# Forget-gate attention by head pairs: row sums by DMA, values held still, S5 and a merge's gates as filler

## The chip, the cores and the metric

The kernel runs on one core of a Trainium2 chip. The core has TensorE (PE, with its weight loads listed apart as PEld), VectorE (DVE), ScalarE (ACT), GpSimd (POOL) and SyncE (SP), which here only issues DMAs. The metric is the time of one execution on the device in microseconds; lower is better.

## The reference, cut to what matters

Two blocks run one after the other on a sequence of 512 tokens with 1024 features. The first block is two hybrid layers, each with neighbourhood attention (NA), grouped-query attention and spatial gating. The second block has forget-gate attention (fox), a state-space mixer (ssd) and a diagonal state-space mixer (S5), merged by gates, and a convolutional feed-forward part.

```python
def neighbourhood_attention(q, k, v, rpb):      # 8 heads of 64, grid 8 x 64
    scores = jnp.einsum('brqhd,brjkhd->bhrqjk', qg, kg) * (dh ** -0.5)
    scores = scores + bias                      # relative bias, window of 16 columns
    p = jax.nn.softmax(jnp.where(col_valid, scores, -1e30))
    out = jnp.einsum('bhrqjk,brjkhd->brqhd', p, vg)
...
def fox_attention(q, k, v, f_logit):            # 8 heads of 64, blocks of 128 queries
    cum = jnp.cumsum(jax.nn.log_sigmoid(f_logit), axis=1)
    for i in range(4):
        s = q[i] @ k[:, :q1].T * scale
        s = s + cum[:, :, q0:q1, None] - cum[:, :, None, :q1]
        p = jax.nn.softmax(jnp.where(causal, s, -inf))
        out = p @ v[:, :q1]
...
merged = sum over the three branches of sigmoid(gate_r + b_gate) * (y_r @ w_branch[r])
```

ssd needs, per head, the exponential of the differences of a running sum within chunks of 128 tokens (`exp(segsum(adt))`) and the exponential of the sum itself. S5 is a complex linear recurrence over the tokens.

## The kernel before, in words

Every large product is made in three parts. An operand is split into a rounded high half and a remainder, and `mm3` (L94) issues high x high (L99), high x remainder (L100, L101) into one PSUM tile. `load_w` (L67) brings a weight tile `wr` by an SP DMA, ScalarE rounds it to `wh` (L76), and DVE or POOL subtracts to get `wl` (L78); which of the two is told by the pattern `lo_gp`, one entry per tile in turn. An `fm_job` makes one output tile of 512 columns in four units of six products; the units wait in a queue and `fill(n)` (L165) takes n of them as filler between the steps of an attention. The tile scheduler then fixes the order on each engine, and each engine works its own queue in order.

NA (`na`, L590) works in 16 steps per layer, one for each pair of heads and 16 columns of queries. A step's scores for two heads are two products against a zero-padded high half of the keys with all 128 rows (L659) and two against the remainder with 64 rows each (L662). The keys of a step are 32 columns of 8 grid rows, taken with a stride. The values of two heads go into the column halves of one PSUM tile (L699).

Block 2 (`block2`, L1479) runs fox, ssd, merges 0, 1 and 2, with S5 (`s5`, L1363) as a generator that is advanced by `step`. RF, RS and RM say how much one call of `step` adds in fox, in ssd and in the merges: 0, 0.5 and 1.5. `fdt` (L829) makes the running sums `CS` of the gates and turns them token-major by small transposes (L862). In fox the 32 steps are one head and one block of 128 queries each. A step's scores are a product with all rows (L941), one with 64 rows (L942) and one that adds the causal mask as a product with the identity (L943). The running sum along the keys is spread over the partitions by a product with one column of the identity (L872, once per head) and copied by ScalarE (L937). A reduction on DVE (L947) subtracts it and finds the maximum; then come the exponential on ScalarE (L952) and the reciprocal on DVE (L953). `weights_T` transposes the weights on PE (L304); the values (L979) hold the transposed weights still and stream 64 columns of `v`, ScalarE scales the result by the reciprocal (L980), and the output of two heads is transposed back to features (L983) and copied (L984). ssd spreads its sums in the same way (L872, with a mask product L1070), and by a product with a selector matrix (L1089). In fox three of four `wl` are made by POOL, in the merges all of them. A merge (`merge_gen`, L716) makes, for each pair of output tiles, two gate jobs and a projection. S5's products with its state are L1438 and L1440, its sums L1394 to L1448. PSUM has three tiles for `mm`, two for `s`, two for `t` and one for `v`.

Of the kernel before, what the change touches and what calls it, by code (L numbers as in the profile page):

```python
# [14 lines left out]
ALU = mybir.AluOpType  # L15
# [10 lines left out]
class Net:  # L26
# [176 lines left out]
    def consts2(self):  # L203
        nc, a, cp = self.nc, self.a, self.cp
        self.identb = cp.tile([P, P], BF16, name="identb")
        nc.vector.tensor_copy(self.identb, self.ident)
        self.identr = cp.tile([P, P], F32R, name="identr")
        nc.vector.tensor_copy(self.identr, self.ident)
# [111 lines left out]
    def heads_k(self, src):  # L320

        nc, out, lo = self.nc, [], self.b2(F32R)
        for s in range(2):
            r, o = slice(64 * s, 64 * s + 64), slice(64 - 64 * s, 128 - 64 * s)
            k = self.b2(F32R)
# [3 lines left out]
            out.append(k)  # L329
        return out, lo  # L330
# [259 lines left out]
    def na(self, l, vd):  # L590
# [12 lines left out]
        def kj(hp):  # L603
            def use(ps):
                kf = self.tmp()
                nc.scalar.activation(kf, ps, AF.Identity, bias=self.col(f"b{l}", 4 + hp))
                kzs[hp] = self.heads_k(kf)
            return self.fm_job(fm[4 + hp], use)
# [14 lines left out]
        def load(hp):  # L623
            vw = [self.b2(shape=(P, 4, P)) for _ in range(2)]
            vr = vd.rearrange("(r c) f -> r c f", c=64)
            for j in range(4):
                for half in range(2):
                    nc.sync.dma_start(vw[j // 2][:, 2 * (j % 2) + half], vr[4 * half:4 * half + 4, LO[j]:LO[j] + 32, hp * P:hp * P + P])
            vws[hp] = vw
            bts[hp] = []  # L630
            for s in range(2):
                t = self.ld(shape=(P, 8, 48))
# [3 lines left out]
        def bias(i):  # L636
# [7 lines left out]
            bms[i] = self.b2(shape=(P, 2, 8, 32))  # L644
            x0 = (16, 8, 8, 0)[j]
            for s in range(2):
                nc.gpsimd.tensor_tensor(bms[i][:, s], bts[hp][s][:, :, x0:x0 + 32],  # L647
                                        self.namask[:, (0, 1, 1, 2)[j], None].to_broadcast([P, 8, 32]), op=ALU.add)

        def weights(hp, j):  # L650
# [12 lines left out]
            for s in range(2):  # L663
                nc.vector.tensor_tensor_reduce(out=e[:, s], in0=pss[s], in1=bm[:, s].rearrange("p r c -> p (r c)"), op0=ALU.add, op1=ALU.max,
# [1061 lines left out]
```

## Time and profile before

| | before |
|---|---|
| median of 3 runs | 2041.87 us (2039.82 to 2045.49) |
| the profiled execution | 2042.89 us |
| its span | 2041.1 us |
| mean granted clock, share of the upper level | 0.991 |
| PE busy | 1988.1 us (97%) |
| DVE, ACT, POOL busy | 1236.0, 863.2, 509.8 us (61%, 42%, 25%) |

The profiled execution has a span of 2041.1 us, and its own time is 1.8 us longer. The two hybrid layers take it to about 1134 us, fox with its head to 1325 us, ssd to about 1380 us, merges 0 and 1 to 1493 us; then come the last merge, the projection and the feed-forward part. A row of the timeline starts with the time from the start of the span; since matmuls are pipelined, what one costs is read from one start to the next.

### The profile page before, as it was taken

The numbers are of one execution on the slowest core, as the hardware profiler recorded it, in microseconds if no ns is written. First come the engines' busy times: TensorE is split into PE (matmuls) and PEld (weight loads), VectorE is DVE, ScalarE is ACT, GpSimd is POOL, SyncE is SP. The second block draws the span as 40 slices with busy tenths as digits, with TensorE's granted clock in tenths as the row PEclk, the third lists the DMA queues.
The fourth block names the chain that finished last, engine by engine and source line by source line (L and its number), as shares of the span: only waits on it lengthen the run. The fifth ranks groups of instructions, "written<-read, shape, count | busy, mean of one in ns | idle before, by whom it ended". The sixth has DMA issues, their size and how long they took to land. (4 is left out here: it accounts for less than half of the span.)

```text
span 2041.1 us, 29326 instructions
## 1 busy us (share of the span) xinstructions
PE 1988.1 (97%) x10594; PEld 1653.3 (81%) x10594; DVE 1236.0 (61%) x2406; ACT 863.2 (42%) x1738; POOL 509.8 (25%) x594
## 2 busy tenths in 40 slices
PE   7999999999999999999999999998899999999998
PEld 7898877788799988777878877877688888888888
DVE  7776655766477766567545644365425477635655
ACT  3445446433235554564332466542233334423431
POOL 3343321100633436323610222235440000000000
PEclk9999999999999999999999999999899999999999
DMA  6432223333352322334353412143433423333332
GB/s 207 153 106 67 80 89 105 109 93 122 117 167 89 105 75 78 124 109 140 107 159 115 140 63 62 62 131 105 138 98 108 130 83 100 102 93 99 98 86 70
DMA packets 140464, 218.54 MB, mean 107 GB/s; under 512 B 19232, under 2 KB 44576, under 8 KB 140320
## 3 DMA queue, kind: packets, MB, share of 16 engines
q1 hardware_dynamic: 140320, 216.68, 33.7%
q8 instruction: 83, 1.36, 0.3%
q14 instruction: 61, 0.50, 0.1%
HBM read 196.70 MB, written 19.92 MB: 106 GB/s over the span
## 5 line engine op out<-in xcount | busy, mean ns | idle before, releaser
L76 ACT CAST wh<-wr 128x512 fp32r<-128x512 f32 x605 | 362.1, 618 | 587.5 <-PE psmm L100 273.7
L99 PE MATMUL psmm<-xh,wh 128*128 128x512 f32 (+1 forms) x1504 | 604.3, 402 | 1.5 <-DVE b L373 1.4
L100 PE MATMUL psmm<-xl,wh 128*128 128x512 f32 (+1 forms) x1504 | 588.1, 391 | 0.3 <-DVE xl L262 0.3
L101 PE MATMUL psmm<-xh,wl 128*128 128x512 f32 (+1 forms) x1504 | 587.4, 391 | 0.2 <-DVE wl L78 0.2
L78 DVE TENSOR_TENSOR wl<-wr,wh 128x512 fp32r<-128x512 f32 x526 | 374.6, 723 | 348.9 <-ACT wh L76 341.4
L101 PEld LDWEIGHTS psmm<-xh,wl 128*128 128x128 f32 x1504 | 283.5, 189 | 61.6 <-DVE wl L78 1.8
L99 PEld LDWEIGHTS psmm<-xh,wh 128*128 128x128 f32 x1504 | 284.1, 189 | 60.8 <-issue 3.4
L100 PEld LDWEIGHTS psmm<-xl,wh 128*128 128x128 f32 x1504 | 284.4, 189 | 52.7 <-DVE xl L262 0.7
L247 POOL TENSOR_TENSOR sm<-sm,mhalf 128x1 f32<-128x1 f32 x20 | 18.9, 947 | 648.4 <-DVE sm L245 648.4
L78 POOL TENSOR_TENSOR wl<-wr,wh 128x512 fp32r<-128x512 f32 x79 | 109.7, 1401 | 229.2 <-ACT wh L76 228.7
L99 PE MATMUL psmm<-wh,xh 128*128 128x256 f32 (+1 forms) x512 | 148.3, 291 | 2.0 <-DVE b L373 1.3
L100 PE MATMUL psmm<-wl,xh 128*128 128x256 f32 (+1 forms) x512 | 147.1, 287 | 2.0 <-DVE wl L78 1.8
L101 PE MATMUL psmm<-wh,xl 128*128 128x256 f32 (+1 forms) x512 | 147.3, 288 | 0.4 <-DVE xl L262 0.4
L465 POOL TENSOR_SCALAR b<-b,sm 128x512 f32<-128x512 f32 x64 | 101.1, 1580 | 163.6 <-DVE sm L296 158.4
L99 PE MATMUL psmm<-b,wh 128*128 128x512 f32 x304 | 119.8, 394 | 0.0
L100 PE MATMUL psmm<-b,wh 128*128 128x512 f32 x304 | 118.6, 390 | 0.0
L101 PE MATMUL psmm<-b,wl 128*128 128x512 f32 x304 | 118.5, 390 | 0.0
L99 PEld LDWEIGHTS psmm<-wh,xh 128*128 128x128 f32 x512 | 99.4, 195 | 4.0 <-DVE b L373 1.7
L100 PEld LDWEIGHTS psmm<-wl,xh 128*128 128x128 f32 x512 | 99.5, 194 | 3.8 <-DVE wl L78 2.6
L101 PEld LDWEIGHTS psmm<-wh,xl 128*128 128x128 f32 x512 | 99.4, 194 | 0.9 <-DVE xl L262 0.9
L647 POOL TENSOR_TENSOR b<-ld,namask 128x256 f32<-128x256 f32 x48 | 42.7, 916 | 151.0 <-PE psv L699 57.3
L294 ACT ACTIVATE b<-pss,sm 128x512 f32<-128x512 f32 x64 | 44.1, 689 | 81.5 <-DVE sm L291 81.0
(393 smaller groups left out, 3304.3 us busy)
## 6 DMA issues: line engine op xcount, KB each, us to landing
wr<-in_w1fm SPq DMA_DIRECT2D x192, 256.0 KB
wr<-in_w2fm SPq DMA_DIRECT2D x92, 256.0 KB
wr<-in_wup SPq DMA_DIRECT2D x88, 256.0 KB
wr<-in_wbr SPq DMA_DIRECT2D x72, 256.0 KB
wr<-in_w1tm SPq DMA_DIRECT2D x56, 256.0 KB
wr<-in_wout SPq DMA_DIRECT2D x48, 256.0 KB
wr<-in_wdown SPq DMA_DIRECT2D x43, 256.0 KB
ld<-in_rows SPq DMA_DIRECT2D x32, 256.0 KB
```

Source lines behind the costliest of these rows:

```text
L76: nc.scalar.copy(hi[:, c], raw)
L78: eng.tensor_tensor(lo[:, c], raw, hi[:, c].bitcast(F32), op=ALU.subtract)
L99: mm(ps, wh, xh, start=(first and k == 0), stop=False)
L100: mm(ps, wh, xl, start=False, stop=False)
L101: mm(ps, wl, xh, start=False, stop=(last and k == n - 1))
L247: nc.gpsimd.tensor_tensor(rs, ve, self.mhalf[:, :1], op=ALU.pow)
L294: nc.scalar.activation(e[:, :n], src, AF.Exp, bias=nm, scale=scale, accum_out=sm)
L465: nc.gpsimd.tensor_scalar(e, e, r, None, op0=ALU.mult)
L647: nc.gpsimd.tensor_tensor(bms[i][:, s], bts[hp][s][:, :, x0:x0 + 32], self.namask[:, (0, 1, 1, 2)[j], None].to_broadcast([P, 8, 32]), op=A ...
```

## The change

NA stores the keys column by column, so that a step's 256 keys lie side by side, and keeps the remainder in both halves of the partitions, so that all four score products have 128 rows. The bias table and the values are laid out to match.

Fox works in 16 steps of two heads. Score products are four with all rows. `CS` is written to memory and spread by DMA (`bcast_row`); POOL subtracts the causal mask from the spread row (`sums`), and after the block on the diagonal has been read, POOL copies the unmasked block over it. The weights are scaled by POOL before they are transposed. The values hold `v` still, 64 columns for each head in the two column halves, and stream the transposed weights, so the output comes out by features. ssd takes its spread rows by DMA and its mask by a POOL addition; the selector product is a DMA to 64 partitions each.

S5 is advanced in fox as well (RF 0.5, from a start of -7) and at 0.5 in merges, with one more stop in it. All `wl` of fox, ssd and merges are made by DVE. The eight gate jobs of merge 0 stand in the filler queue during ssd, and are drained before merge 0. The jobs in fox are put in another order: S5's inputs early, the convolutions (`xj`) late.

```diff
-        nc, out, lo = self.nc, [], self.b2(F32R)
+        nc, out = self.nc, []
         for s in range(2):
             r, o = slice(64 * s, 64 * s + 64), slice(64 - 64 * s, 128 - 64 * s)
-            k = self.b2(F32R)
+            k, lo = self.b2(F32R), self.b2(F32R)
             nc.scalar.copy(k[r], src[r])
             nc.scalar.copy(k[o], src[r])
             nc.vector.tensor_tensor(lo[r], src[r], k[r].bitcast(F32), op=ALU.subtract)
-            out.append(k)
-        return out, lo
+            nc.scalar.copy(lo[o], lo[r].bitcast(F32))
+            out.append((k, lo))
+        return out
...
-            vr = vd.rearrange("(r c) f -> r c f", c=64)
+            vr = vd.rearrange("(r c) f -> c r f", c=64)
             for j in range(4):
                 for half in range(2):
-                    nc.sync.dma_start(vw[j // 2][:, 2 * (j % 2) + half], vr[4 * half:4 * half + 4, LO[j]:LO[j] + 32, hp * P:hp * P + P])
+                    c0 = LO[j] + 16 * half
...
-            jq = slice(j * P, j * P + P)
-            q, (ks, kl) = [x[:, jq] for x in qs[hp]], kzs[hp]
-            ks, (kl,) = ([x.rearrange("p (r c) -> p r c", c=64)[:, :, LO[j]:LO[j] + 32] for x in xs] for xs in (ks, (kl,)))
+            jq, jk = slice(j * P, j * P + P), slice(8 * LO[j], 8 * LO[j] + 256)
             pss = [self.psum("s", (P, 256)) for _ in range(2)]
             for s in range(2):
-                nc.tensor.matmul(pss[s], q[s], ks[s], start=True, stop=False)
+                for i, k in enumerate(kzs[hp][s]):
+                    nc.tensor.matmul(pss[s], qs[hp][s][:, jq], k[:, jk], start=(i == 0), stop=(i == 1))
             for s in range(2):
-                r = slice(64 * s, 64 * s + 64)
-                nc.tensor.matmul(pss[s], q[s][r], kl[r], start=False, stop=True)
...
-        js, ts = [], {}
+        js, done, ts = [], ts, ts or {}
 
...
         for dp in range(4):
-            js += [gj(2 * dp), gj(2 * dp + 1), pj(dp)]
+            js += ([] if done else [gj(2 * dp), gj(2 * dp + 1)]) + [pj(dp)]
         yield from self.jobs(js)
+
+    def gate_job(self, ts, dt, r, gates, bname, b0, buf):
+        def use(ps):
+            ts[dt] = buf()
+            self.nc.scalar.activation(ts[dt], ps, AF.Tanh, bias=self.hcol(bname, b0 + 8 * r + dt), scale=0.5)
+        return self.fm_job(gates(8 * r + dt), use)
...
+        self.csd = self.dr.tile([40, 512], F32, name="csd")
+        nc.sync.dma_start(self.csd, CS[0:40])
+        yield
...
+    def bcast_row(self, out, r):
+
+        self.nc.sync.dma_start(out, self.csd[r:r + 1].to_broadcast([out.shape[0], 512]))
...
-        js += [uj(F) for F in range(4)]
+        js += [xj(0), qj(1), kj(1), uj(0), uj(1), qj(2), kj(2), xj(1), uj(2), qj(3), kj(3), uj(3), xj(2), xj(3), xj(4), xj(5)]
+        js += [zj(i) for i in range(4)]
         self.queue.append(self.jobs(js))
         self.fill(12)
+        fdt = self.fdt(fd)
+        next(fdt)
+        self.lo_gp = (0,)
         self.fill(8)
+        next(fdt)
+        steps = [(hp, t) for hp in range(4) for t in range(4)]
...
+        def sums(hp):
+
+            cks[hp] = []
+            for s in range(2):
+                c, m = self.b2(), self.b2()
+                self.bcast_row(c, 2 * hp + s)
+                nc.gpsimd.tensor_tensor(m.rearrange("p (t q) -> p t q", t=4), c.rearrange("p (t q) -> p t q", t=4),
+                                        self.causal[:, None].to_broadcast([P, 4, P]), op=ALU.subtract)
+                cks[hp].append((c, m))
+        sums(0)
+        self.fill(6)
...
+            pss = [self.psum("s") for _ in range(2)]
+            es = [self.b2() for _ in range(2)]
+            for s in range(2):
+                qt, (kh, kl) = q[hp][s][:, t * P:t * P + P], kz[hp][s]
+                nc.tensor.matmul(pss[s][:, :nn], qt, kh[:, :nn], start=True, stop=False)
+                nc.tensor.matmul(pss[s][:, :nn], qt, kl[:, :nn], start=False, stop=True)
+
+            mx, nm, sm, r = (self.small(2) for _ in range(4))
+            for s in range(2):
+                c, m = cks[hp][s]
+                nc.vector.tensor_tensor_reduce(out=es[s][:, :n], in0=pss[s][:, :n], in1=m[:, :n], op0=ALU.subtract, op1=ALU.max,
+                                               scale=1.0, scalar=-3e38, accum_out=mx[:, s:s + 1])
+                if t < 3:
+                    nc.gpsimd.tensor_copy(m[:, n - P:n], c[:, n - P:n])
+            cq = self.cc[:, t, 2 * hp:2 * hp + 2]
+            nc.vector.scalar_tensor_tensor(nm, mx, -1.0, cq, op0=ALU.mult, op1=ALU.subtract)
             nc.vector.tensor_tensor(nm, nm, cq, op=ALU.add)
-            nc.scalar.activation(e[:, :n], e[:, :n], AF.Exp, bias=nm, accum_out=sm)
+            for s in range(2):
+                nc.scalar.activation(es[s][:, :n], es[s][:, :n], AF.Exp, bias=nm[:, s:s + 1], accum_out=sm[:, s:s + 1])
             nc.vector.reciprocal(r, sm)
-            return e, r
+            for s in range(2):
+                nc.gpsimd.tensor_scalar(es[s][:, :n], es[s][:, :n], r[:, s:s + 1], None, op0=ALU.mult)
+            return es
...
+                sc[i] = weights(hp, t)
+            self.fill(1)
+            step(1)
             self.fill(1)
             step(1)
             j = i - 1
             if 0 <= j < len(steps):
-                pes[j] = self.weights_T(sc[j][0], steps[j][1] + 1)
+                pes[j] = [self.weights_T(e, steps[j][1] + 1) for e in sc.pop(j)]
             self.fill(1)
             step(1)
             j -= 1
...
-                nc.scalar.mul(yt[:, s], po[:, s], sc.pop(j)[1])
-                if s:
-                    pt = self.psum("t", (P, P))
-                    nc.tensor.transpose(pt, yt.rearrange("p s d -> p (s d)"), self.ident)
-                    nc.scalar.copy(ys[hp][:, t * P:t * P + P], pt)
-                    if t == 3:
-                        self.d(f"fox_{hp}", ys[hp])
+                    for s in range(2):
+                        h = 2 * hp + s
+                        nc.tensor.matmul(po[64 * s:64 * s + 64], v[k][:, h * 64:h * 64 + 64], pe[s][:, k], start=(k == 0), stop=(k == t))
+                nc.scalar.copy(ys[hp][:, t * P:t * P + P], po)
...
+        def sums(j):
+
+            out = [self.b2() for _ in range(3)]
+            for s in range(2):
+                self.bcast_row(out[s], 32 + 2 * j + s)
+                nc.gpsimd.tensor_tensor(out[s], out[s], self.causalT, op=ALU.add)
+                self.bcast_row(out[2][64 * s:64 * s + 64], 32 + 2 * j + s)
+            return out
+        nxt = sums(0)
...
-        due = [0.0]
+        due = [-7.0]
...
+        self.queue.append(self.jobs([self.gate_job(ts, dt, 0, lambda i: a["w2fm"][22 + i], "bg", 0, self.b2) for dt in range(8)]))
         yb = self.ssd(xb, zz, lambda n: step(RS))
+        self.fill(drain=True)
         tags[:] = "s", "t"
-        self.lo_gp = (1,)
-        merge(0, ya, RM, first=True)
+        merge(0, ya, RM, first=True, ts=ts)
         merge(1, yb, RM)
...
-RF = 0.0
+RF = 0.5
 RS = 0.5
-RM = 1.5
+RM = 0.5
```

On PE in a fox step, before: the values of one head (L979), then its scores (L941 to L943) and, two filler products later, the output transpose (L983).

```order
L101 MATMUL psmm_13081<-xh_11669,wl_12881 128x512
L979 MATMUL psv_13099<-acc_76,b_2833_13091 128x64
L979 MATMUL psv_13099<-acc_77,b_2833_13091 128x64
L941 MATMUL pss_13148<-b_2762_12846,b_2735_12751 128x512
L942 MATMUL pss_13148<-b_2761_12845,b_2735_12751 128x512
L943 LDWEIGHTS identb
L943 MATMUL pss_13148<-causalb,identb 128x128
L99 MATMUL psmm_13172<-xh_11669,wh_12982 128x512
L100 MATMUL psmm_13172<-xl_11670,wh_12982 128x512
L983 MATMUL pst_13145<-ident,yt_13100 128x128
L101 MATMUL psmm_13172<-xh_11669,wl_12983 128x512
```

After, at the like place: scores of two heads in four full products (L950, L951); further on S5's output products (L1454, L1456), the two heads' transposes (L300) and their values side by side (L996).

```order
L950 MATMUL pss_13181<-b_2723_12731,b_2700_12651 128x512
L951 MATMUL pss_13181<-b_2724_12732,b_2700_12651 128x512
L950 MATMUL pss_13182<-b_2725_12737,b_2701_12654 128x512
L951 MATMUL pss_13182<-b_2726_12738,b_2701_12654 128x512
L99 MATMUL psmm_13164<-xh_11689,wh_12946 128x512
...
L1454 MATMUL psmm_13222<-b_2746_12816,ld_12985 128x128
L1456 MATMUL psmm_13222<-b_2811_13071,ld_12981 128x127
L1456 MATMUL psmm_13222<-b_2812_13072,ld_12982 128x127
L300 MATMUL pst_13241<-ident,b_2821_13088 128x128 x2
L300 MATMUL pst_13247<-ident,b_2822_13089 128x128 x3
L996 MATMUL psv_13270<-b_2836_13147,acc_76 64x128
L996 MATMUL psv_13270<-b_2838_13152,acc_76 64x128
```

The scores stand together, the mask product and the output transpose are gone, and S5's products stand inside the loop. Transposes of both heads stand together too.

On DVE in the last head pair of fox, before: the reduction (L947), the small instructions (L950 to L953), and little between them.

```order
L947 ISA b_3055_13870,sm_13871<-pss_13866,b_3001_13690 128x384
L947 ISA sm_13871 128x1
L950 TENSOR_SCALAR sm_13872<-sm_13871,cc 128x1
L951 TENSOR_TENSOR sm_13872<-sm_13872,cc 128x1
L953 RECIPROCAL sm_13874<-sm_13873 128x1
L914 SCALAR_TENSOR_TENSOR b_3062_13898<-tmp_13899,psmm_13843 128x512
L947 ISA b_3066_13912,sm_13913<-pss_13908,b_2984_13634 128x512
L947 ISA sm_13913 128x1
L950 TENSOR_SCALAR sm_13914<-sm_13913,cc 128x1
```

After: the reductions (L956), small instructions (L961, L962, L965) with convolution sums (L1012, L904), S5's sums (L1440, L1441) and a `wl` between them.

```order
L956 ISA b_3031_13919,sm_13925<-pss_13917,b_2924_13499 128x384
L956 ISA sm_13925 128x1
L904 SCALAR_TENSOR_TENSOR b_3014_13856<-tmp_13861,b_3014_13856 128x512
L956 ISA b_3032_13920,sm_13925<-pss_13918,b_2926_13503 128x384
L956 ISA sm_13925 128x1
L1440 TENSOR_TENSOR b_3039_13960<-b_3002_13815,ld_13560 128x512
L961 SCALAR_TENSOR_TENSOR sm_13926<-sm_13925,cc 128x2
L1012 SCALAR_TENSOR_TENSOR b_3037_13952<-psmm_13892,hcols,b_3037_13952 128x511
L962 TENSOR_TENSOR sm_13926<-sm_13926,cc 128x2
L1441 TENSOR_TENSOR b_3041_13962<-b_3004_13817,ld_13561 128x512
L1012 SCALAR_TENSOR_TENSOR b_3037_13952<-psmm_13892,hcols,b_3037_13952 128x510
L78 TENSOR_TENSOR wl_13978<-wr_13979,wh_13977 128x512
```

Between two pairs' reductions DVE now has some ten other large instructions, where before it had none or one.

On PE in merge 1, before: the wait for S5 lies here, at L1440 among products of the merge.

```order
L100 MATMUL psmm_15086<-xl_11670,wh_14997 128x512
L101 MATMUL psmm_15086<-xh_11669,wl_14998 128x512
L1440 MATMUL pst_14843<-b_3278_14801,ld_14785 128x127
L99 MATMUL psmm_15086<-xh_11669,wh_14997 128x512
L100 MATMUL psmm_15086<-xl_11670,wh_14997 128x512
L101 MATMUL psmm_15086<-xh_11669,wl_14998 128x512
L99 MATMUL psmm_15086<-xh_11669,wh_14997 128x512
L1440 MATMUL pst_14843<-b_3279_14802,ld_14786 128x127
L1438 MATMUL pst_14843<-b_3150_14258,ld_14789 128x128
L1440 MATMUL pst_14843<-b_3278_14801,ld_14785 128x127
```

After: S5's last products (L1456) stand in ssd, beside its own (L1111); further on merge 0 begins with three tiles at once behind the last gate job.

```order
L1101 MATMUL pst_14543<-b_3157_14437,b_3133_14371 64x128
L1101 MATMUL pst_14543<-b_3158_14438,b_3133_14371 64x128
L1454 MATMUL psmm_14560<-b_2962_13637,ld_14255 128x128
L1456 MATMUL psmm_14560<-b_3147_14410,ld_14251 128x127
L1456 MATMUL psmm_14560<-b_3148_14411,ld_14252 128x127
L1111 MATMUL pst_14580<-b_3154_14426,st_14291 64x128 x2
...
L100 MATMUL psmm_14915<-xl_11690,wh_14851 128x512
L101 MATMUL psmm_14915<-xh_11689,wl_14852 128x512
L99 MATMUL psmm_14988<-b_3234_14942,wh_14958 128x512
L99 MATMUL psmm_15002<-b_3234_14942,wh_14958 128x512
L99 MATMUL psmm_15026<-b_3234_14942,wh_14968 128x512
```

S5's products moved from the merges to fox and ssd.

## Rows read from the trace of the kernel before

**Rows 1.** The page, busy time of each engine over the span.

```profile
PE 1988.1 (97%) x10594; PEld 1653.3 (81%) x10594; DVE 1236.0 (61%) x2406; ACT 863.2 (42%) x1738; POOL 509.8 (25%) x594
```

**Rows 2.** PE's waits: line <- releaser: us in total, times, longest us.

```profile
PE pst L1440 <- POOL b L1427: 15.7, 3, 6.2
...
PE pst L862 <- DVE b L859: 3.6, 1, 3.6
```

**Rows 3.** Windows: S5 wait in merge 1, a full-DVE stretch, fox loop.

```profile
core 0: us, PE busy (x) PEld busy (x) DVE busy (x) ACT busy (x) POOL busy (x), PEclk, DMA share, GB/s
1424.00:1437.00 13.00, 6.78 (x31) 5.64 (x31) 9.52 (x8) 0.53 (x2) 8.47 (x6) 0.74 0.42 136
...
403.00:433.00 30.00, 30.00 (x151) 23.84 (x150) 28.17 (x88) 13.11 (x22) 0.21 (x2) 1.00 0.28 83
...
1170.00:1325.00 155.00, 153.91 (x798) 120.14 (x796) 67.06 (x212) 94.08 (x229) 33.35 (x26) 1.00 0.19 58
```

**Rows 4.** Timeline of PE, one step of neighbourhood attention: start us, us, instruction.

```profile
338.41 0.40 PE L101 MATMUL psmm<-xh,wl 128*128 128x512 f32 x1
338.74 0.66 PE L699 MATMUL psv<-b,b 128*64 128x128 f32 x8
339.33 0.51 PE L659 MATMUL pss<-b,b 128*128 128x256 f32 x2
339.77 0.39 PE L662 MATMUL pss<-b,b 64*128 64x256 f32 x2
340.08 0.50 PE L99 MATMUL psmm<-xh,wh 128*128 128x512 f32 x1
```

**Rows 5.** Timeline of PE, one fox step with 384 columns.

```profile
1229.38 0.56 PE L979 MATMUL psv<-acc,b 128*128 128x64 f32 x4
1229.74 0.42 PE L941 MATMUL pss<-b,b 128*128 128x384 f32 x1
1230.09 0.44 PE L942 MATMUL pss<-b,b 64*128 64x384 f32 x1
...
1230.50 0.48 PE L99 MATMUL psmm<-xh,wh 128*128 128x512 f32 x1
1230.81 0.40 PE L100 MATMUL psmm<-xl,wh 128*128 128x512 f32 x1
```

**Rows 6.** Timeline of PE, broadcast of a row sum in fox.

```profile
1172.39 0.63 PE L872 MATMUL pss<-b,identr 128*128 128x512 f32 x2
1172.86 0.39 PE L99 MATMUL psmm<-xh,wh 128*128 128x512 f32 x1
```

**Rows 7.** Timeline of PE, broadcast and mask in ssd.

```profile
1340.29 0.71 PE L872 MATMUL pss<-b,identr 128*128 128x512 f32 x2
1340.84 0.39 PE L1070 MATMUL pss<-causalTb,identb 128*128 128x512 bf16 x1
1340.88 0.58 PE L99 MATMUL psmm<-xh,wh 128*128 128x512 f32 x1
1341.30 0.39 PE L100 MATMUL psmm<-xl,wh 128*128 128x512 f32 x1
```

**Rows 8.** Lines on DVE by form, 1134 to 1500 us: busy us, mean ns | idle before.

```profile
L951 DVE TENSOR_TENSOR sm<-sm,cc 128x1 f32<-128x1 f32 x32 | 6.9, 214 | 0.9
...
L1430 DVE TENSOR_TENSOR b<-b,ld 128x512 f32<-128x512 f32 x4 | 5.9, 1480 | 0.0
...
L1394 DVE SCALAR_TENSOR_TENSOR b<-b,b 128x512 fp32r<-128x512 f32 x4 | 4.9, 1218 | 16.6 <-ACT b L1393 16.6
...
L1448 DVE SCALAR_TENSOR_TENSOR b<-b,b 128x512 f32<-128x512 f32 x4 | 2.8, 693 | 2.2 <-ACT b L1447 2.1
...
L1429 DVE TENSOR_TENSOR b<-b,ld 128x512 f32<-128x512 f32 x4 | 2.7, 680 | 0.0
```

**Rows 9.** Lines by form, 100 to 200 us, on POOL and on DVE.

```profile
L465 POOL TENSOR_SCALAR b<-b,sm 128x512 f32<-128x512 f32 x18 | 28.2, 1569 | 39.2 <-DVE sm L296 39.2
...
L78 DVE TENSOR_TENSOR wl<-wr,wh 128x512 fp32r<-128x512 f32 x26 | 18.1, 710 | 1.9 <-ACT wh L76 1.7
```

More of the change, by code (lines that the diff above doesn't have):

```diff
@@ L714, in merge, with merge_gen @@
         return out
-    def merge_gen(self, out, r, ys, wbr, gates, bname, b0, first=False, last=False, step=None):
+    def merge_gen(self, out, r, ys, wbr, gates, bname, b0, first=False, last=False, step=None, ts=None):
         nc = self.nc
@@ L865, in fdt @@
         nc.vector.tensor_copy(cc, pc)
-        self.CSr, self.cc = self.split(CS), cc
-    def bcast_row(self, ps, r, last=True):
-        one = self.identr[:, r:r + 1].to_broadcast([P, P])
-        for i in range(2):
-            self.nc.tensor.matmul(ps, one, self.CSr[i], start=(i == 0), stop=(i == 1 and last))
+        self.cc = cc
+        yield
+    def bcast_row(self, out, r):
+        self.nc.sync.dma_start(out, self.csd[r:r + 1].to_broadcast([out.shape[0], 512]))
     def fox(self, xb, zz, step):
@@ L915, in zj @@
             return self.fm_job(fm[8 + i], use)
-        js += [zj(i) for i in range(4)]
         def uj(F):
@@ L920, in fox @@
         self.ub = {}
-        js += [uj(F) for F in range(4)]
+        js += [xj(0), qj(1), kj(1), uj(0), uj(1), qj(2), kj(2), xj(1), uj(2), qj(3), kj(3), uj(3), xj(2), xj(3), xj(4), xj(5)]
+        js += [zj(i) for i in range(4)]
         self.queue.append(self.jobs(js))
         self.fill(12)
-        self.fdt(fd)
-        self.lo_gp = (1, 1, 1, 0)
+        fdt = self.fdt(fd)
+        next(fdt)
+        self.lo_gp = (0,)
         self.fill(8)
-        steps = [(hp, t, s) for hp in range(4) for t in range(4) for s in range(2)]
@@ L955, in fox @@
+            return es
         for i in range(len(steps) + 2):
             if i < len(steps):
-                hp, t, s = steps[i]
+                hp, t = steps[i]
                 while kz[hp] is None:
                     self.fill(1)
-                sc[i] = weights(hp, t, s)
+                if t == 2 and hp < 3:
+                    sums(hp + 1)
+                sc[i] = weights(hp, t)
+            self.fill(1)
+            step(1)
             self.fill(1)
@@ L1065, in ssd @@
                 mt = []
+                *pbs, e = nxt
+                nxt = sums(j + 1) if j < 3 else None
                 for s in range(2):
                     h = 2 * j + s
-                    pb = self.psum("s")
-                    self.bcast_row(pb, 32 + h, last=False)
-                    nc.tensor.matmul(pb, self.identb, self.causalT, start=False, stop=True)
-                    m = self.b2()
+                    m = pbs[s]
                     for c in range(4):
-                        nc.scalar.activation(m[:, c * P:c * P + P], pb[:, c * P:c * P + P], AF.Exp, bias=ncs[:, c, h:h + 1])
+                        nc.scalar.activation(m[:, c * P:c * P + P], m[:, c * P:c * P + P], AF.Exp, bias=ncs[:, c, h:h + 1])
                     nc.vector.tensor_tensor(m, m, cb, op=ALU.mult)
@@ L1086, in ssd @@
                 step(1)
-                pe = self.psum("s")
-                for i in range(2):
-                    nc.tensor.matmul(pe, pselr[:, j * P:j * P + P], self.CSr[i], start=(i == 0), stop=(i == 1))
-                e = self.b2()
-                nc.scalar.activation(e, pe, AF.Exp)
+                nc.scalar.activation(e, e, AF.Exp)
                 po = self.psum("t")
@@ L1434, in s5 @@
             yield
+            yield
             py = self.psum(tags[1])
@@ L1610, in _constants @@
     c["rst"] = r
-    ps = np.zeros((P, S), np.float32)
-    for j in range(4):
-        for s in range(2):
-            ps[32 + 2 * j + s, j * P + 64 * s:j * P + 64 * s + 64] = 1
-    c["psel"] = ps
     return c
```

76 lines of the change are left out of this document (24 added, 52 removed).

## The prediction

> **What bounds the kernel now.** I read the engine totals first, then what TensorE (PE) waited for, then busy time stretch by stretch, then single rows of PE's timeline. PE is busy for 1988.1 of 2041.1 us [rows 1]; every other engine has slack on the whole. So only two things can pay: less work on PE, or less waiting of PE. The waits are few [rows 2]: three waits of the S5 output products (L1440) for GpSimd (POOL), 15.7 us together, and one of the transposes in `fdt` (L862), 3.6 us. The stretch around one of the S5 waits shows that they cost more than they last: of 13 us PE worked 6.78, and its mean granted clock was 0.74 of the upper level, 2.4 GHz [rows 3]. In the forget-gate (fox) loop, 1170 to 1325 us, PE is full (153.91 of 155), while VectorE (DVE) is busy for 67.06 and POOL for 33.35 [rows 3]. That DVE slack is what the change spends.
>
> **The sum is made against the profiled execution**, 2042.9 us with a span of 2041.1; the median of the runs is 2041.9, so the profiled one stands 1 us high, which I neglect. What follows is in PE time, since PE is the end of nearly every stretch.
>
> **Neighbourhood attention, 32 steps (16 in each of two layers).** A step's scores take 0.44 us for the two products with all 128 rows (339.33 to 339.77), 0.31 for the two with 64 rows [rows 4], and the product after a 64-row one takes 0.31 [rows 5] instead of the 0.23 that 512 columns cost in an unbroken stream (0.47 for two [rows 6]): 0.83 us. After, four full products of 256 columns: at half of 0.23 each, so 0.46 by columns, and about 0.10 for coming out of the column-split value products, which is inside today's 0.44. That is 0.56, a gain of 0.27 a step and **8.8 us** in all. The extra copy of the low half falls to ScalarE, which works a small part of any such stretch. If that copy came late it would cost once per head pair, not per step: 8 times some 0.6 us at most, and I take nothing.
>
> **`fdt`.** Its transposes now stand eight products later in PE's order: 8 x 0.23 = 1.8 us of its 3.6 us wait go [rows 2, 6]. A shorter wait also costs less clock afterwards; by the S5 stretch a wait cost up to 13 x 0.26 = 3.4 us of it [rows 3], and I count half of that. **3.4 us** between 1.8 and 7.
>
> **Fox, scores.** A step for one head with 384 columns: 0.35 for the full product (1229.74 to 1230.09), 0.41 to the next ordinary product and 0.08 more in that [rows 5], 0.84 us; by the same reading 0.73 with 256 columns and 0.96 with 512. 16 x 0.73 + 8 x 0.84 + 8 x 0.96 = 26.1 us. After: 16 head pairs with four full products each, 16 x 4 x mean 0.16 us (columns in proportion to 0.23 for 512) = 10.2. Gain **15.9**.
>
> **Fox, values.** Today 160 small products at close to 0.1 each (four in 0.36 [rows 5], a little more in longer rows), 15.3 us, and 16 output transposes with the slower product behind them, 1.8. After, the two heads run abreast, as today's L699 does: eight products in 0.59 us, of which some 0.15 are entering and leaving [rows 4], so 160 in 8.8, and 16 entries and exits at 0.2 (a product before L699 holds the array for 0.33 instead of 0.23 [rows 4], and leaving costs the like), 3.2. Gain 17.1 - 12.0 = **5.1**. Head pairs also halve the places where softmax transposes interrupt the stream, 16 x 0.09 = **1.4**.
>
> **Row sums.** Eight pairs of broadcast products at 0.47 [rows 6] leave fox, **3.8**. In the state-space part (ssd) eight pairs at 0.55 go, eight mask products that make the next one 0.42 instead of 0.23, and four pairs of selector products: 4.4 + 1.9 + 2.0 = **8.3** [rows 7]. What replaces them is DMA on SyncE's queue and POOL work; 24 transfers there stand among weight loads, and DMA is busy at 0.19 in the fox loop [rows 3], so I take no cost for the bytes. The first pair hangs on a chain (write, read back, POOL subtraction), but some forty filler products (9 us) stand between the `fdt` transposes and the first use.
>
> **The S5 tail.** S5's generator is now advanced 29 times in fox and 8 times in ssd, 37 for the 36 stops that it has, and in PE's order its last product stands ahead of the merges. So the three waits of 15.7 us go with their clock: 15.7 at least, 15.7 + 3 x 3.4 = 25.9 at most [rows 2, 3]. I take **24**, since PE was busy for most of the slow time that followed. PE's own S5 work is moved, not removed.
>
> The gains: 8.8 + 3.4 + 15.9 + 5.1 + 1.4 + 3.8 + 8.3 + 24 = **70.7 us**.
>
> **What it puts on other engines.** In fox, DVE takes over the weight remainders that POOL made: POOL's 26 instructions there are nearly all such, some 23 x 0.73 = 17 us. The S5 groups of lines L1394 to L1448 add up to 54.7 us for 37 steps (the first and the last of 17 groups and two more stand in [rows 8]), and 29 of the steps come here: 43. Half of the small instructions per head fall away, 32 at 0.21 (L951 and its neighbour [rows 8]) and 16 reciprocals at a little less, so -9. 67 + 17 + 43 - 9 = **118 us of DVE** (counting each instruction in the new order by its duration gives 116) against PE's 118 (155 less 26, less the fill that the earlier head took, plus S5's products). ScalarE loses some of its copies and stays below both. POOL has some 71: 32 scalings at 1.57 per 512 columns [rows 9], masks, copies and S5's part. So DVE, half idle today, becomes level with PE. It runs its queue in order; behind a reciprocal that waits for ScalarE's exponentials stand the next scores' reduction, a convolution and weight remainders, and for these PE waits. In the last head pair three steps put 34 us on DVE and 21 on PE, since the convolutions are bunched there.
>
> A precedent is at 403 to 433 us: DVE busy for 28.17 of 30 and PE for 30.00 [rows 3]. So a full DVE need not stop PE, if the order is good. Bounds for the new waits: 0 by this precedent, and 40 by the second rival below. I take 10 in fox (two thirds of the 13 us by which the last pair overhangs), 3 in ssd, where DVE gets S5's remainder and the gate jobs' remainders (54 us against PE's 58), and 2 before merge 0, whose input splits on DVE stand behind a filler's weight remainder: **15 us**. The gate jobs of merge 0 themselves are moved and cost nothing twice.
>
> 2042.9 - 70.7 + 15 = **1987 us**.
>
> **Rival one, no new waits.** If the precedent holds throughout, 2042.9 - 70.7 = 1972, and with the whole `fdt` wait gone 1969.
>
> **Rival two, DVE and POOL hinder each other.** The rows leave room for it: the same DVE sum takes 0.68 (L1429) and 1.48 right behind it, where POOL's add L1427 runs beside (L1430) [rows 8]. They also show a pair that does not: while POOL scales 128x512 tiles, remainders on DVE take 0.71 [rows 9]. The scalings are the largest part of POOL's new work, so I lean to the second. If all of POOL's 71 us in fox delayed DVE for the share of its time that goes to sums of two tiles in SBUF (52 of 116 us), DVE gained 32 us of work and the loop lasted 148 instead of 118 + 10; with 8 us more in ssd and 2 at the merge the new waits are 40: 2042.9 - 70.7 + 40 = 2012. The Trainium skill has this as a rule (SBUF — State Buffer, "Who interferes with whom"): a DVE instruction with two SBUF inputs contends with a GpSimd instruction that reads SBUF, and the one that comes second blocks for the whole of the other. By that the scalings would block too; the 0.71 us of rows 9 speaks against it, the 1.48 of rows 8 for it.
>
> **Rival three, slower: the softmax chain of a pair comes late at every step.** Reductions, exponentials, reciprocal, POOL scaling and transposes now all lie between one pair's scores and its transposes, and today's scaling sat behind the values instead. With 512 columns the chain is 0.77 x 2, 0.4, 0.9 x 2, 0.2 and 1.57 x 2: 7 us, against an iteration of 118/16 = 7.4 and two filler units. If queues in front of each step make PE late by x us in all 16 steps, and each wait loses 1.7 us of clock (half of the 3.4 above), the new waits are 16 (x + 1.7) + 5. The gain is eaten at x = 2.4; at x = 3.2 it would be 16 x 4.9 + 5 = 83, so 2055 us. Against it speaks that fillers are spread between the steps and that today's loop, with a similar chain, leaves PE idle for 1.1 us in 155 [rows 3].
>
> **Rival four, the S5 tail stays.** The order excludes it as far as PE's rows go; if S5's steps were slowed so that their products reached the merges, 24 us less: 2011, which lies with rival two.
>
> **Chances.** Forecast (new waits of 8 to 28 us, 1980 to 2000) 0.5; rival one 0.2; rivals two and four 0.22; three 0.08, half of it beyond the old time. About 0.3% (6 us) can be told from no change: faster 0.91, same 0.04, slower 0.05. The range for 8 in 10 leaves out the slow end of rivals two and three and the best end of one: 1966 to 2016, the terms' bounds included (clock of the tail 2 us, `fdt` 3.6 us).
>
> **What would show it.** Right: no PE wait at L1440's successor (L1456) in the merges; scores of a fox pair as four rows with ordinary products behind them at 0.23; the fox loop at 125 to 135 us with PE over 90% and DVE over 85%; remainders on DVE at 0.75 or less beside POOL's scalings. Rival two: remainders or S5 sums well over 1 us in fox and PE waiting for L78. Rival three: PE waiting for POOL's scaling ahead of the transposes at most steps, with granted clocks under 0.9 in fox. I am wrong if the neighbourhood step gains less than 0.2 us, or if the readback of row sums stops PE ahead of the first score reduction.

## The result, and the profile after

The changed kernel takes 1992.84 us (median of 4 runs, 1988.93 to 1994.96) against 2041.82 us: a ratio of 0.9756, 95% interval 0.9735 to 0.9777, 49 us less. 1987 was forecast, 1966 to 2016 the range. The profiled execution took 1994.96 us, with a span of 1993.1, 48.0 less than before.

The page after, busy time of each engine, answers [rows 1]:

```profile
PE 1944.5 (98%) x10498; PEld 1626.0 (82%) x10498; DVE 1264.8 (63%) x2433; ACT 864.0 (43%) x1721; POOL 465.4 (23%) x587
```

PE's waits between 1150 and 1420 us (line <- releaser: us in total, times, longest us) answer [rows 2]:

```profile
PE pst L300 <- POOL b L967: 4.8, 6, 1.3
PE pss L1052 <- POOL b L1049: 4.1, 3, 3.1
PE psmm L1456 <- POOL b L1446: 2.1, 2, 1.1
PE psmm L99 <- ACT b L87: 1.6, 1, 1.6
...
PE pst L863 <- DVE b L857: 0.9, 1, 0.9
```

The S5 tail is gone: L1456, the line that was L1440, costs 2.1 us in fox instead of 15.7 in the merges. `fdt` waits 0.9 us (L863) instead of 3.6. What is new is small and spread: transposes that wait for the scaling on POOL (L300 for L967), ssd's state products for the decay product on POOL (L1052 for L1049), merge 0's first product for the rounding of its input (L87).

Windows after, the fox loop and ssd (us, then busy us of PE, PEld, DVE, ACT, POOL, granted clock, DMA share, GB/s), answer the fox row of [rows 3]:

```profile
1164.00:1322.00 158.00, 149.32 (x858) 119.19 (x858) 107.54 (x226) 89.91 (x206) 78.83 (x83) 0.99 0.43 133
1322.00:1390.00 68.00, 61.44 (x387) 47.01 (x386) 48.87 (x76) 29.23 (x68) 23.61 (x19) 1.00 0.45 121
```

DVE went from 67 to 108 us and POOL from 33 to 79. PE, which had 1.1 us of idle time in fox, has 8.7 there and 6.6 in ssd. The loop is 158 us long with its last values and the filler behind them; from the first to the last score product it is 132.6 us, with 8.2 us of PE idle and DVE busy for 91.2. So the 125 to 135 us of the forecast hold for that shorter stretch alone, and DVE, at 68 or 69% by either measure, is not level with PE.

A step of neighbourhood attention after (start us, us, instruction), against [rows 4]:

```profile
336.56 0.40 PE L101 MATMUL psmm<-xh,wl 128*128 128x512 f32 x1
336.89 0.66 PE L694 MATMUL psv<-b,b 128*64 128x128 f32 x8
337.47 0.73 PE L657 MATMUL pss<-b,b 128*128 128x256 f32 x4
338.04 0.40 PE L99 MATMUL psmm<-xh,wh 128*128 128x512 f32 x1
338.28 0.40 PE L100 MATMUL psmm<-xl,wh 128*128 128x512 f32 x1
```

The four products take 0.57 us (337.47 to 338.04), and the next product takes 0.24 with no delay: 0.56 was forecast.

**Where the 48 us came from.** The ordinary products of PE come in the same order in both traces up to fox, and again from the last merge on, so their starts can be compared one by one. Behind the last score product of neighbourhood attention the new kernel is 9.1 us ahead; behind `fdt` and the slow clock that follows it 13.1; at the start of the last merge 48.0, and from there to the end the two run alike. So 35 us come from fox, ssd and merges 0 and 1.

### The profile page after: what moved, and what is told of

Read it like the earlier page. It is cut to its first block, busy times and chain, and to the rows that moved or that the text cites. A ratio compares the mean times of both kernels' runs of the same rounds, so it can differ in the third digit from the quotient of the medians.

```text
span 1993.1 us, 29239 instructions
## 1 busy us (share of the span) xinstructions
PE 1944.5 (98%) x10498; PEld 1626.0 (82%) x10498; DVE 1264.8 (63%) x2433; ACT 864.0 (43%) x1721; POOL 465.4 (23%) x587
## 5 line engine op out<-in xcount | busy, mean ns | idle before, releaser
L78 DVE TENSOR_TENSOR wl<-wr,wh 128x512 fp32r<-128x512 f32 x605 | 434.8, 730 | 409.1 <-ACT wh L76 397.4
L99 PE MATMUL psmm<-xh,wh 128*128 128x512 f32 (+1 forms) x1504 | 596.4, 397 | 3.6 <-DVE b L370 1.4
L646 POOL TENSOR_TENSOR b<-ld,namask 128x256 f32<-128x256 f32 x48 | 35.4, 765 | 153.7 <-PE pst L300 57.4
L99 PEld LDWEIGHTS psmm<-b,wh 128*128 128x128 f32 x304 | 57.0, 188 | 13.8 <-ACT b L87 2.0
```

What stands on the lines that cost most here:

```text
L78: eng.tensor_tensor(lo[:, c], raw, hi[:, c].bitcast(F32), op=ALU.subtract)
L99: mm(ps, wh, xh, start=(first and k == 0), stop=False)
L646: nc.gpsimd.tensor_tensor(bms[i][:, s], bts[hp][s][:, x0:x0 + 32], self.namask[:, (0, 1, 1, 2)[j], :, None].to_broadcast([P, 32, 8]), op=A ...
```

## The experiments

Eleven kernels were run. Each is given against runs of the kernel before on the same chip (2041.0, 2041.5 and 2042.6 us in the three sessions); 1992.8 is the changed kernel. Its own four runs lie 6 us apart and it was timed in one session alone, so differences from it are good to some 3 us, and their tenths mean nothing.

### Neighbourhood attention alone

The new `na`, `heads_k` and bias layout on the kernel before; fox keeps its product with 64 rows:

```diff
-            qt, (ks, kl) = q[hp][s][:, t * P:t * P + P], kz[hp]
+            qt, (ks, kl) = q[hp][s][:, t * P:t * P + P], kz[hp][s]
```

> The neighbourhood-attention part alone on the kernel before (keys column by column, remainder in both halves, four full products a step; fox keeps its 64-row product). Forecast, by the trace of after (32 steps, 0.27 us each): 2041.8 - 8.6 = 2033, 2030 to 2036. Rival, that the step's gain is only seen because the rest changed (other queues late): no gain, 2039 to 2043.

Measured 2034.66 us against 2040.95, ratio 0.9967 (0.9956 to 0.9977), 6.3 us by medians; the profiled spans differ by 8.5 us (2041.1 and 2032.6). The interval is 4.7 to 9.0 us less, so the forecast of 8.6 lies within it, near its end: the part stands by itself.

### S5 in the merges again

```diff
-        due = [-7.0]
+        due = [0.0]
...
-RF = 0.5
+RF = 0.0
...
-RM = 0.5
+RM = 1.5
```

> After, but S5 is stepped as before (RF 0, start 0, RM 1.5): its products go back to the merges. Theory of the forecast: the tail of 16.4 us idle and 7.6 us of clock returns, and of the 20 us of new waits in fox and ssd most go, since S5's sums leave POOL and DVE: 1993 + 24 - 14 = 2003, 1998 to 2010. Rival: the new waits are not S5's but the scaling's and the masks', and stay: 2013 to 2017.

Measured 2013.54 us: the rival's 2013 to 2017. Its waits from 1140 to 1480 us:

```profile
PE pst L1456 <- POOL b L1442: 20.9, 3, 13.2
PE pst L300 <- POOL b L967: 5.4, 7, 1.3
PE pst L1101 <- DVE b L1093: 4.1, 3, 2.1
```

With S5 out of fox the transposes still wait 5.4 us for the scaling; it was 4.8 with S5. So these waits are not S5's. And S5's tail costs more than it did (20.9 us, 15.7 before), since merge 0 has no gate jobs between its products any more: with the gate jobs back in merge 0, in a run further on, it is 11.9.

### The scaling on VectorE

```diff
-                nc.gpsimd.tensor_scalar(es[s][:, :n], es[s][:, :n], r[:, s:s + 1], None, op0=ALU.mult)
+                nc.vector.tensor_scalar(es[s][:, :n], es[s][:, :n], r[:, s:s + 1], None, op0=ALU.mult)
```

> After, but the softmax weights of fox are scaled by VectorE instead of GpSimd, one word changed. Theory A, that the new waits come from GpSimd's queue (scalings behind S5's sums and the masks): the waits of the transposes go, about 8 us, 1983 to 1988. Theory B, that VectorE is the full engine: its 32 scalings of some 0.4 to 0.7 us come on top, PE waits longer, 1998 to 2010.

Measured 1988.49 us, 4.3 less, just outside theory A's numbers (by half a us) and well off theory B's. The scaling by form, first on POOL in the changed kernel, 1134 to 1500 us (busy us, mean ns | idle before):

```profile
L967 POOL TENSOR_SCALAR b<-b,sm 128x512 f32<-128x512 f32 x8 | 13.2, 1664 | 17.2 <-DVE sm L965 17.2
...
L967 POOL TENSOR_SCALAR b<-b,sm 128x256 f32<-128x256 f32 x8 | 10.5, 1319 | 7.5 <-DVE sm L965 5.9 <-PE psv L996 1.6
```

then on DVE in this run, 1160 to 1313 us:

```profile
L967 DVE TENSOR_SCALAR b<-b,sm 128x512 f32<-128x512 f32 x8 | 3.5, 482 | 0.1
...
L967 DVE TENSOR_SCALAR b<-b,sm 128x256 f32<-128x256 f32 x8 | 2.4, 344 | 0.1
```

What POOL does in 1.66 us, DVE does in 0.48, so the 32 scalings cost DVE 10.8 us, where 0.4 to 0.7 us each, as theory B has it, would be 13 to 22. DVE goes to 114 us of the 153 in that window and PE waits for it at L300 only 1.1 us.

### Weight remainders on POOL again

```diff
-        self.lo_gp = (0,)
+        self.lo_gp = (1, 1, 1, 0)
         self.fill(8)
```

> After, but three of four weight remainders in fox, ssd and the merges are made by GpSimd, as before in fox. Theory A (GpSimd's queue): some 50 instructions of 1.4 us more stand in front of scalings and S5's sums, so later: 2003 to 2025. Theory B (VectorE is full): relief, 1983 to 1989.

Measured 2007.24 us, 14.4 more, in theory A's range, but only in part by its cause. PE waits 4.3 us for S5's sum on POOL (L1446; 2.1 in the changed kernel), and `fdt`'s wait is 4.6 us (0.9), but the waits of the transposes for the scaling fall from 4.8 to 3.0 us, where theory A has them grow. The mean granted clock over the span goes from 0.995 to 0.991. How the 14.4 us divide was not separated. So it was needed that `wl` left POOL; relief for VectorE brought nothing.

### The gate jobs in merge 0 again

```diff
-        self.queue.append(self.jobs([self.gate_job(ts, dt, 0, lambda i: a["w2fm"][22 + i], "bg", 0, self.b2) for dt in range(8)]))
...
-        merge(0, ya, RM, first=True, ts=ts)
+        merge(0, ya, RM, first=True)
```

> After, but the eight gate jobs of merge 0 are made in merge 0 again and not as filler in ssd. Theory of the prediction (a gate job is moved and costs nothing twice; ssd has enough other filler): 1990 to 1996. Rival: without them ssd has too few ordinary products between its own steps (8 jobs of 24 products, 44 us), and what S5 and ssd wait for on VectorE and GpSimd shows on TensorE: 2003 to 2025.

Measured 2004.11 us: the rival. The end of ssd, waits and windows:

```profile
PE pss L1130 <- ACT b L1125: 4.3, 1, 4.3
...
PE pst L1111 <- DVE b L1103: 1.7, 1, 1.7
PE pst L1137 <- POOL sm L1134: 1.3, 1, 1.3
```

```profile
1365.00:1385.00 20.00, 12.56 (x91) 11.00 (x91) 11.90 (x20) 10.04 (x20) 1.70 (x2) 0.66 0.29 80
1385.00:1400.00 15.00, 15.00 (x61) 12.66 (x61) 8.70 (x15) 3.35 (x6) 1.39 (x1) 0.77 0.07 22
```

Fox now takes 72 filler units instead of 68 and has six more ahead of its loop, so ssd's last chain (square, sum, root, transposes) has nothing beside it. PE stands for 7.4 us of 20, and the granted clock falls to 0.66 and 0.77 of the upper level on average. PE's idle time in the whole span grew by 7.1 us (48.6 to 55.7, span less busy time); the rest of the 11.3 is the clock, as far as the rows tell (0.995 to 0.991 on average).

### S5's shift alone

On the kernel before:

```diff
-        due = [0.0]
+        due = [-5.0]
...
-RF = 0.0
+RF = 0.5
...
-RM = 1.5
+RM = 0.5
```

with the new order of jobs and the additional stop in S5.

> S5's shift alone on the kernel before: steps of 0.5 in fox from a start of -5 (27 to 29 of the 36 stops fall in fox), the new order of jobs, one more stop; scores, values, row sums, remainders on GpSimd and gate jobs stay as before. If the shift pays by itself, as the prediction counts it: 2041 - 24 + 5 of new waits = 2022, 2017 to 2028. Rival: with GpSimd's remainders of weights in front of S5's sums the waits come back inside fox: 2032 to 2042.

Measured 2032.76 us, 8.7 less than before: the rival by its number, but not by its cause. The waits:

```profile
PE psmm L1407 <- DMA b<-usd: 4.5, 1, 4.5
PE pst L862 <- DVE b L859: 3.6, 1, 3.6
PE pst L1121 <- POOL sm L1118: 2.1, 1, 2.1
PE pss L1036 <- POOL b L1033: 2.0, 3, 1.1
```

The tail is gone, as forecast, and PE's waits for S5's sums didn't come back in fox. S5's first product waits instead for the read-back of its input, 4.5 us, with a mean clock of 0.83 in the 20 us around it; and ssd's end waits at L1121. How much of the missing 11 us to the forecast of 2022 lies in this run's own start (-5 where the changed kernel has -7, in a loop of other length) was not separated.

### The scaling on VectorE, S5 in the merges

Both edits shown above, of S5 and of the scaling.

> s5_back with the scaling on VectorE: S5 in the merges, no scaling on GpSimd. If the waits ahead of the transposes are the scaling's own time on GpSimd, with or without S5 (5.4 us in s5_back and about 3 hidden between transposes): 2013.5 - 8 = 2005, 2003 to 2008. If they come from the length of the softmax chain wherever the scaling runs: 2011 to 2015.

Measured 2009.24 us, 4.3 less than with the scaling on POOL (2013.54), the same 4.3 as with S5 in fox. The waits at L300 for the scaling shrink from 5.4 to 0.4 us and PE waits in ssd for L1093 a little more (5.0 instead of 4.1). So the scaling's place is worth some 4 us, whatever S5 does (the same tenth twice is chance); of my 8 the other half wasn't there.

### S5 and the gate jobs both as before

The edits of the two runs that undo one each.

> After with both undone: S5 stepped as before and the gate jobs of merge 0 in merge 0, so attention and row sums alone are changed. If the two parts add (20.7 us and 11.3 us in the runs that undo one): 1993 + 32 = 2025, 2021 to 2029. If the gate jobs help ssd only because S5 is in it, and in merge 0 they give S5's tail its filler back (in s5_back PE waited 20.9 us at L1456 where the kernel before waited 15.7): 2006 to 2013.

Measured 2009.55 us: the parts don't add. Undoing S5's shift costs 20.7, undoing the gates 11.3, undoing both 16.7. The two belong together, since gate jobs are filler either for S5's tail in merge 0 or for ssd. With S5 in fox they are worth 11.3 us in ssd; with S5 in the merges they are worth 4.0 us more in merge 0 (2013.54 less 2009.55), where PE's wait at S5's products is 11.9 us with them and 20.9 without. All the rest of the change brings 2042.6 - 2009.6 = 33 us: attention and row sums, and with them the remainders on VectorE, the new order of jobs and `fdt`'s later place, which this run keeps.

### The values as before

```diff
-                po = self.psum("v", (P, P))
+                po = self.psum("v", (P, 2, 64))
...
-                        nc.tensor.matmul(po[64 * s:64 * s + 64], v[k][:, h * 64:h * 64 + 64], pe[s][:, k], start=(k == 0), stop=(k == t))
-                nc.scalar.copy(ys[hp][:, t * P:t * P + P], po)
+                        nc.tensor.matmul(po[:, s], pe[s][:, k], v[k][:, h * 64:h * 64 + 64], start=(k == 0), stop=(k == t))
+                nc.scalar.copy(yt, po)
+                pt = self.psum("t", (P, P))
+                nc.tensor.transpose(pt, yt.rearrange("p s d -> p (s d)"), self.ident)
+                nc.scalar.copy(ys[hp][:, t * P:t * P + P], pt)
```

> After, but fox's values hold the transposed weights still and stream 64 columns of v, one head after the other, with an output transpose and one more ScalarE copy, as before. By the prediction's term for the values (17.1 - 12.0): 1993 + 5 = 1998, 1996 to 2000. If what counts there are waits and not PE's work (the values behind late transposes): 1991 to 1995.

Measured 1997.90 us, 5.1 more: the term of the prediction (17.1 - 12.0). PE's waits are nearly those of the changed kernel and its busy time goes from 1944.5 to 1949.4 us, so it is PE's work that costs, and not waits. The agreement to the tenth is luck: in PE's rows after the change the values take 12.2 us themselves and make ordinary products before and behind them 0.33 and 0.34 us long instead of 0.23, so that by the rows 2 to 3 us are gained.

### Two faster versions

The first takes three kinds of instruction from POOL to DVE:

```diff
-                nc.gpsimd.tensor_scalar(es[s][:, :n], es[s][:, :n], r[:, s:s + 1], None, op0=ALU.mult)
+                nc.vector.tensor_scalar(es[s][:, :n], es[s][:, :n], r[:, s:s + 1], None, op0=ALU.mult)
...
-            nc.gpsimd.tensor_tensor(xe, xd, de[:, c, :, None].to_broadcast([P, 8, 64]), op=ALU.mult)
+            nc.vector.tensor_tensor(xe, xd, de[:, c, :, None].to_broadcast([P, 8, 64]), op=ALU.mult)
...
-            gp.tensor_tensor(zi, zi, t3, op=ALU.add)
+            v.tensor_tensor(zi, zi, t3, op=ALU.add)
```

> After with three sums or products taken from GpSimd to VectorE: the scaling, ssd's decay product ahead of its states (3 instructions of 1.46 us, PE waits 4.1 us for them) and S5's last sum (4 of 1.55 us, PE waits 2.1). Theory A (GpSimd's slow instructions stand in the chains that PE waits for, VectorE has room): 1988.5 - 4 = 1984, 1982 to 1987. Theory B (VectorE is near its limit with the scaling): 1988 to 1995.

Measured 1985.48 us, theory A. The second adds

```diff
+        ya = [self.split(y) for y in ya]
         self.fill(drain=True)
```

> v2 (scaling, decay product and S5's last sum on VectorE) with the four input splits of merge 0 written ahead of the drained filler jobs, so that they don't stand behind the last weight remainders. If the 1.6 us wait at the start of merge 0 goes with no new one: 1985.5 - 2 = 1983.5, 1982 to 1985. If the last gate jobs then wait for the splits on ScalarE and VectorE: 1985 to 1988.

Measured 1982.08 us, ratio to before 0.9697 (0.9681 to 0.9713), 10.8 us less than the changed kernel. Its largest waits between 1140 and 1480 us:

```profile
PE pst L1101 <- DVE b L1093: 1.7, 2, 1.0
PE psmm L99 <- DVE b L324: 1.4, 2, 1.1
PE pss L1052 <- DVE b L1049: 1.3, 1, 1.3
PE psv L996 <- ACT b L302: 1.2, 1, 1.2
```

No wait is over 1.7 us in all, and DVE is busy for 117.28 us of 153 in fox: the room for it was there.

## Why the prediction was right, point by point

**The sign, the size and the bound were right.** PE was the bound and stayed it; 70.7 us of gains less new waits gave 55.7 where 48.0 were measured by the spans. Most of the 7.7 us between them lies in two terms.

**The new waits, taken at 15 us, are the first: about 20.** From `fdt` to the end of merge 1 PE is idle for 16.8 us, 14.3 more than before without the tail. The 80 transposes of weights take 10.1 us from start to start instead of 6.2, and behind the waits at 1290 us the granted clock is at its lower level for 3.4 us, which costs 1.7. That the idle time alone comes near 15 is luck, for the step behind the 15 was wrong. I put the new waits down to a full DVE: "DVE, half idle today, becomes level with PE". The instruction count was nearly right (116 to 118 us, 107.5 measured in the loop), but I set it against 118 us of PE as if both filled the same stretch. From the first to the last score product PE took 132.6 us, 8.2 of them idle, and DVE worked 91.2 us there; the rest of its work lies beside the last values and the filler. DVE had 50 us of room in 158. Taking work off DVE (the remainders, to POOL) made it 14.4 us slower; giving it POOL's scaling, 10.8 us of work, made it 4.3 us faster.

At the transposes it is the length of the scaling on POOL that counts, two heads one after the other, more than POOL's queue: in 14 of the 16 pairs the first scaling starts within 0.2 us of the end of the reciprocal. PE waits in four pairs, six times. The place with the longest of these waits, in fox's last pair of heads, is one of the two where POOL is late; POOL and DVE in the changed kernel:

```profile
1284.75 1.29 POOL L1431 TENSOR_TENSOR b<-b,b 128x512 f32<-128x512 f32 x1 [0.33 <-DVE sm L961]
1286.80 1.30 POOL L1432 TENSOR_TENSOR b<-b,b 128x512 f32<-128x512 f32 x1 [0.76 <-PE pss L951]
1287.31 1.87 DVE L1437 TENSOR_TENSOR_SCAN b<-b,b 128x512 f32<-128x512 f32 x1
1288.07 3.60 POOL L967 TENSOR_SCALAR b<-b,sm 128x256 f32<-128x256 f32 x2
1289.74 1.21 DVE L1437 TENSOR_TENSOR_SCAN b<-b,b 128x512 f32<-128x512 f32 x1
```

and PE there:

```profile
1289.96 0.44 PE L300 MATMUL pst<-ident,b 128*128 128x128 f32 x2 [0.51 <-POOL b L967]
...
1291.73 0.53 PE L300 MATMUL pst<-ident,b 128*128 128x128 f32 x2 [1.33 <-POOL b L967]
```

The reciprocal is ready at 1287.4 us, POOL is at S5's sum until 1288.07, and then two scalings, 1.8 us each, release one head's transposes after the other. A scaling of 256 columns takes 0.92 us at its fastest (two in 1.82 us at 1177.48); here DVE runs S5's scan beside it. PE was ready at 1289.45 and 1290.40. At 0.92 us each the scalings would have ended at 1288.99 and 1289.91, so by this working these 1.8 us of waits go with rival two. The other 2.9 us, in three pairs of sixteen, are rival three's chain on a small scale.

The longest wait of all stands in ssd, and there DVE's queue has its part:

```profile
1325.80 0.38 PE L1040 MATMUL pst<-ident,b 128*128 128x128 f32 x2
1325.89 1.30 POOL L1432 TENSOR_TENSOR b<-b,b 128x512 f32<-128x512 f32 x1
1325.97 2.30 DVE L1437 TENSOR_TENSOR_SCAN b<-b,b 128x512 f32<-128x512 f32 x1 [0.71 <-POOL b L1431]
1328.19 0.66 DVE L1042 TENSOR_TENSOR b<-pst,cc 128x512 f32<-128x512 f32 x1
1328.99 1.82 POOL L1049 TENSOR_TENSOR b<-b,de 128x512 f32<-128x512 f32 x1 [1.81 <-DVE b L1042]
1329.90 1.46 DVE L78 TENSOR_TENSOR wl<-wr,wh 128x512 fp32r<-128x512 f32 x1
1330.87 0.65 PE L1052 MATMUL pss<-b,b 128*64 128x256 f32 x4 [3.05 <-POOL b L1049]
```

The transposes (L1040) end at 1326.18, but L1042, which reads them, stands behind S5's scan until 1328.19; only then come POOL's decay product and PE's state products. With S5 stepped as before, PE waits 1.2 us at L1052 in all instead of 4.1.

**The scores in fox are the second: 15.9 us forecast, 13.9 found.** The four products of a pair took 11.1 us in all (a wait of 0.6 behind one of them left out) and not 10.2, and the 22.6 of the kernel before with 2.5 us in the products behind them and not 26.1: the reading of one step with 384 columns [rows 5] was carried over to the others a little too high. The values (5.1 forecast, 5.1 in the run that undoes them), the broadcasts and masks (12.1 forecast, 12.0 from start to start) and neighbourhood attention (8.8 forecast, though 32 times 0.27 is 8.6; 9.1 by PE's starts) were right. The 1.4 us for fewer interruptions by transposes came as 1.8 in the products behind them, and the transposes' own rows took back more than twice that.

**The S5 tail came out as forecast, its price did not.** The 16.4 us of waits and 7.6 us of clock (PE worked for some 15 us at the lower level there) are gone. "The gate jobs of merge 0 themselves are moved and cost nothing twice" was half of it: without them in ssd the kernel is 11.3 us slower with S5 in fox. I had looked at what they cost and not at what ran empty without them.

**`fdt`** had 2.7 of its 3.6 us back and not 1.8, and some of the clock with it: 4.0 us (9.1 ahead in front of it, 13.1 behind), 3.4 forecast.

**Rival two.** DVE and POOL do hinder each other here. A remainder (`wl`) on DVE with no POOL instruction beside it takes 0.69 us. Seven of the loop's 35 start while POOL adds or subtracts two full tiles (L937, L1442, L1446), and each of them ends 0.55 us after that instruction does, wherever it began; so does the one at 1329.90 above, where POOL ends at 1330.81 and the remainder at 1331.36. So the one that comes second waits for the other's end. Beside POOL's scalings it is mostly not so: of the eight remainders that start during one, five take 0.68 or 0.69 us and the slowest 1.02. The rule of the Trainium skill (SBUF — State Buffer, "Who interferes with whom") names two inputs from SBUF against a GpSimd instruction that reads, the loser blocked for the whole of the other. This trace agrees for POOL's sums of two tiles (0.55 us seven times of seven) and not for most remainders beside scalings, which read SBUF too. The loss is small because few come second: 35 remainders at 0.87 instead of 0.69 are 6.4 us, where the prediction's 32 let all of POOL's time hold DVE. The sign of 0.75 us or less was missed all the same: 0.87 on average, 0.77 without the scaling on POOL and 0.78 without S5, where 0.71 was read in [rows 9]. The other way round, POOL's scaling of 256 columns takes 1.32 us on average with S5 beside it and 0.98 without (s5_back).

The row of the remainders in the changed kernel, 1164 to 1322 us:

```profile
L78 DVE TENSOR_TENSOR wl<-wr,wh 128x512 fp32r<-128x512 f32 x35 | 29.8, 869 | 17.9 <-ACT wh L76 14.3 <-PE pst L300 3.4
```

**What stays open.** With the scaling on DVE 2.6 of the 3.9 us by which the weights' transposes grew are still there. About half of that is grouping: 64 of the 80 transposes are followed by another one (0.11 us to its start), 48 before, and 10 by an ordinary product (0.03), 32 before. Six are followed by values in the column halves, 0.20 us each. No run separated these. S5's shift alone brought 8.7 us where 19 were expected, for a reason of its own in that run. No run undid the scores or the row sums alone: what they brought rests on PE's rows.

## What to carry to other kernels

Price PE's products from one start to the next, entries and exits of a tile mode included: such terms came out within 2 us here, most within a few tenths. When work moves to another engine, ask not how full that engine gets on the whole, but which of its instructions PE's chain passes through, how long they take there, and what they wait for or run beside; a slow engine that is half empty holds up more than a fast one at three quarters. Filler that is moved is missed where it was taken from: look at what is left there with nothing beside it.

## What the runs showed of the hardware that I had not expected

- Scaling 128x512 f32 by a column takes 0.48 us on DVE (x8) and 1.57 to 1.66 us on POOL; 128x128 takes 0.28 and 0.61 to 0.65. From these, DVE's price per column is about a fifth of POOL's, while for a sum of two tiles it is about half (0.68 and 1.30).
- Two heads' products in column halves, eight instructions in 0.58 us (336.89 to 337.47 above), need 0.10 us more on either side. Four score products of which two had 64 rows took 0.83 us a step with the slower product behind them; with 128 rows each and as many columns they take 0.57.
- A remainder on DVE that starts during a POOL sum of two tiles ends 0.55 us after that sum, ten times of ten between 1134 and 1450 us, and so takes up to 1.78 us instead of 0.69. S5's scan, 1.21 us alone, ends 1.08 us after it, four times of four. DVE instructions with one input in PSUM (L956, L1093) take their usual 0.67 to 0.69 us beside the same sums.
- A wait of 4.3 us at the end of ssd (gates_back) and 3 us of shorter ones near it left the mean granted clock at 0.66 and 0.77 of the upper level in the 35 us around them.
